# Mixing stage of a hybrid decoder block: norm sums placed among the u products, masks added once per bank, zero rows by DMA, a new order of steps

## The chip, the cores and the metric

One core of a Trainium2 chip runs the whole kernel in one launch. The metric is device time in microseconds of that core; less is better. TensorE multiplies, VectorE and ScalarE work on elements, GpSimd does some element work and issues DMAs, SyncE only issues DMAs. Each engine runs its own queue in order and waits on semaphores of the others.

## The reference

One layer of a decoder block on 512 tokens of width 1024, in float32, cut to what matters:

```python
h = h + 0.5 * swiglu(rmsnorm(h, norm_ffn1), w1, w3, w2)
z = rmsnorm(h, norm_mix) @ w_in          # q | k, v of three branches | gates | u
o = concat(nsa(q, k, v, gates), s5(u))   # attention of 8 heads, and a state-space mixer on u
h = h + o @ w_out
h = h + 0.5 * swiglu(rmsnorm(h, norm_ffn2), ...)
h = h + sigmoid(rmsnorm(h) @ w_gate) * (p @ w_ple)
out = rmsnorm(h, norm_final)
```

The attention has three branches over the same queries: compressed keys (31 blocks, made from k and v by a small network), selected blocks and a window. With 512 tokens the last two both see all earlier tokens, so each is a causal softmax over keys of its own. The three are weighted by gates. The S5 mixer is a linear recurrence over time in 32 groups of 16 channels.

## The kernel before

Activations lie transposed, features on the 128 partitions and the 512 tokens along the free axis. Each float32 product is made of three products of rounded parts (`hi`, `lo` of the weights, `xh`, `xl` of the activations). Weights come in units of 128 x 1024 from `wpack`, through a ring `raw` of four buffers. ScalarE casts a unit to `hi`, VectorE subtracts it for `lo` (`split`, line 143), and the ring of `hi` and `lo` has three buffers each. A unit of the input projection is 24 products of 512 columns (`proj`, line 745).

The first feed-forward layer ends with eight sums of `down`. Each adds into `h`, and `Norm.feed` (line 183) then makes `xh`, `xl` and the running sum of squares `acc` for the next norm. The norm itself is `rsqrt_steps` (line 256). TensorE sums `acc` over the partitions into a bank D; VectorE and GpSimd take the root (`ms`, `ri`, `nt`, with GpSimd's power); VectorE makes four diagonals `dg`; TensorE spreads them with `ones` into another bank D; VectorE copies that to `rb` (line 190). The norm's factor is applied after the projection, so u, q and k can be multiplied before it is known, as far as PSUM banks hold them: tags A to D, two banks each.

`mixer` (line 696) holds the mixing stage, about 378 to 662 us. It is made of generators, one for each strand of work:

- `s5_input` (u): four u units, finished with `rb` into `ut`, stored, and read back as `u8`
- `rotary` (q, Q, and in `keys` for k): two units, six VectorE operations in the single buffers `r1`, `rb1`, `r2`, `r3`, then two stores. `keys` reads the stored keys back as `kf` (two buffers under the tag `ra`, which other tiles share) and makes `KA` and `KB`
- `s5_all` (s): the recurrence, chunk by chunk; `s5_back` transposes pairs of chunks and copies them to `yt`
- `cmp_kv` (z), `cmp_all` (c): the compressed keys and values, stored, read back in windows (`cst`) and multiplied with their weights
- `v_gates` (v), `glu` (g), `out_half` (f, half of the output projection)
- `queries` (p): reads q of one block of 128 queries back as `qf` and makes `QA` and `QB`, whose rows 64 to 111 hold the row maxima later and zeros at first
- `scores` (t), `compressed` (x): scores with queries on the partitions, for maxima and sums. Keys are added by two products (`KA`, `KB`); a third, with the identity `identb` as the stationary operand, adds the mask (line 1069)
- `values` (V): scores again with keys on the partitions, exponentials, products with the values

`PLAN` (line 1355) is a list of letters. Each takes the next piece of its strand, and a digit names the query block. This sets the order in which pieces are written down. A scheduler then orders each engine's queue by estimated times, except for instructions that are pinned (`pinned`, line 123). `issue_after` keeps one instruction behind another.

Where the lines below need a letter of a table: `TQ` (line 1346) names the banks of q's products, `GT` the buffers of the gelu, which are `r1` and `r2` again.

Of the kernel before, what the change touches and what calls it, by code (L numbers as in the profile page):

```python
# [10 lines left out]
F32 = mybir.dt.float32  # L11
# [4 lines left out]
OP = mybir.AluOpType  # L16
# [60 lines left out]
def block_kernel(ctx: ExitStack, tc: tile.TileContext, a: dict, out: bass.AP):  # L77
# [618 lines left out]
    def mixer(ctx):  # L696
# [22 lines left out]
        nc.scalar.dma_start(w2, a["cmp_w2"])  # L719
        bglu = mp.tile([128, 4], F32, name="bglu")  # L720
        nc.scalar.dma_start(bglu, a["b_glu"])
        G.tensor_scalar(bglu, bglu, 0.5, None, OP.mult)

        for br in range(2):
            V.tensor_copy(KB[64:112, 2 * br:2 * br + 2, :],
                          orow[:, br + 1:br + 2, None].to_broadcast([48, 2, SEQ]))
        zero = mp.tile([128, 1], F32, name="zero")
        pad(mp, PADS[1])
        G.memset(zero, 0.0)
        tp = ctx.enter_context(tc.tile_pool(name="tmp", bufs=1, reuse_waits="tile"))  # L730
        s5x = ExitStack()
        s5w = s5x.enter_context(tc.tile_pool(name="s5w", bufs=2, reuse_waits="tile"))
        V.tensor_copy(KBc[64:112], orow[:, 0:1].to_broadcast([48, 160]))
        V.tensor_copy(VLc.rearrange("p g d -> p (g d)"), zero[:, 0:1].to_broadcast([128, 256]))
        V.tensor_copy(KAc, zero[:, 0:1].to_broadcast([128, 192]))
        V.tensor_copy(KBc[0:64], zero[0:64, 0:1].to_broadcast([64, 160]))


        at = {}
# [27 lines left out]


        def s5_input():
            for m in range(4):  # L770
                o = proj("u", TU[m % 2])
                if m == 0:
                    nm.finish()
                    for t, raw in zip((cosr, sinr), ropes):
                        V.tensor_tensor(t, raw, nm.rb, OP.mult)
                ut = mp.tile([128, 8, 64], F32, tag="ut", name="ut", bufs=2)
                V.tensor_tensor(ut.rearrange("p s c -> p c s"), o.rearrange("p (c s) -> p c s", s=8),
                                nm.rb.rearrange("p (c s) -> p c s", s=8), OP.mult)
                nc.sync.dma_start(ud[128 * m:128 * (m + 1)], ut)
# [253 lines left out]
        def queries(qb, pool):  # L1033

            tq = slice(qb * 128, (qb + 1) * 128)
            QA = pool.tile([128, 8, 128], FR, tag="QA", name="QA", bufs=2)
            QB = pool.tile([128, 8, 128], FR, tag="QB", name="QB", bufs=2)
            envs[qb].update(QA=QA, QB=QB)
            S.copy(QB[64:112].rearrange("p h q -> p (h q)"), zero[64:112, 0:1].to_broadcast([48, 1024]))
            for i, (hs, st) in enumerate(zip((slice(0, 4), slice(4, 8)), STAGE[qb])):  # L1040
                src = qd[i].rearrange("(h r) a t -> (r a) h t", h=4)[:, :, tq]
                if st == "ra":
                    qf = mp.tile([128, 4, 128], F32, tag=st, name="qf", bufs=2)
                else:
                    qf = tp.tile([128, 4, 128], F32, tag=st, name="qf")
                nc.sync.dma_start(qf[0:64], src)
                nc.sync.dma_start(qf[64:128], src)
                S.activation(QA[:, hs], qf, AF.Copy, scale=0.125)
                S.activation(QB[0:64, hs], qf[0:64], AF.Copy, scale=0.125)
                V.scalar_tensor_tensor(QA[64:128, hs], qf[64:128], 0.125, QA[64:128, hs].bitcast(F32),  # L1050
                                       OP.mult, OP.subtract)
                yield

        def scores(qb, tags="B"):

            nk = (qb + 1) * 128
# [292 lines left out]
GT = "r1", "r2"
# [2 lines left out]

PLAN = """u u u k u s s k s k s s s q q Q s k s Q s p3 t3 t3 s z t3 s s t3 z s t3 s s t3 t3 s p3 t3 s t3 g t3 g t3 t3 v
g v c t3 v c v c c c c p2 t2 t2 p2 t3 c t2 t3 t2 c t2 t3 c v t2 c t2 t2 t2 t2 t2 t2 t2 t2 g t2 t2 close p1 p1
p0 p0 x3 g g g g t1 t1 x2 S2 R3 V3 V3 V3 V3 V3 V3 f t1 t1 R2 t1 f t1 f x1 t1 V3 V3 V3 V3 V3 f V3 V3 V3 f t1 V3
V3 V3 V3 t0 V3 V2 f V2 t0 V2 V2 t0 V2 V2 t0 V2 V2 x0 f V2 V2 S0 R1 V2 R0 V2 V2 V2 f V2 V1 V1 V1 V1 V1 V1 V1 V1
V1 V1 V1 V0 V0 V0 V0 V0 V0 V0"""
DEBUG_STOP = None  # L1360
PADS = 320, 0, 224, 24832

# [150 lines left out]
```

## Time and profile before

| | us |
|---|---|
| median of three runs | 1076.79 (1075.64 to 1078.86) |
| the profiled execution's own time | 1076.96 |
| its span, first to last instruction | 1075.2 |
| TensorE busy in the span | 1042.5 |
| VectorE, ScalarE, GpSimd busy | 756.0, 459.4, 170.5 |

The span lies 1.8 us under the time of the same execution. PE in a row is TensorE's products, PEld its weight loads, DVE is VectorE, ACT ScalarE, POOL GpSimd, SP SyncE. A group of rows names the view it is from.

### The profile page before, as it was taken

The numbers are of one execution on the slowest core, as the hardware profiler recorded it, in microseconds if no ns is written. First come the engines' busy times: TensorE is split into PE (matmuls) and PEld (weight loads), VectorE is DVE, ScalarE is ACT, GpSimd is POOL, SyncE is SP. The second block draws the span as 40 slices with busy tenths as digits, with TensorE's granted clock in tenths as the row PEclk, the third lists the DMA queues.
The fourth block names the chain that finished last, engine by engine and source line by source line (L and its number), as shares of the span: only waits on it lengthen the run. The fifth ranks groups of instructions, "written<-read, shape, count | busy, mean of one in ns | idle before, by whom it ended". The sixth has DMA issues, their size and how long they took to land.

```text
span 1075.2 us, 14929 instructions
## 1 busy us (share of the span) xinstructions
PE 1042.5 (97%) x5782; PEld 872.3 (81%) x5782; DVE 756.0 (70%) x1271; ACT 459.4 (43%) x778; POOL 170.5 (16%) x191
## 2 busy tenths in 40 slices
PE   7999999999999989899999999999999999999995
PEld 5888888888888868676587668799899899899885
DVE  6995454545447857587678876997598679687666
ACT  6222223124222531337767865554256245245441
POOL 4006065425549411000000000000000000000000
PEclk9999999999999999998999999999999999999998
DMA  7333225326933938764612014333333323423402
GB/s 253 124 99 101 95 98 156 107 92 205 220 102 112 294 98 219 217 205 135 210 40 59 1 39 137 99 110 108 97 101 101 133 71 107 137 79 121 151 23 79
DMA packets 50391, 132.66 MB, mean 123 GB/s; under 512 B 10560, under 2 KB 17312, under 8 KB 50320
## 3 DMA queue, kind: packets, MB, share of 16 engines
q10 hardware_dynamic: 26080, 90.51, 26.5%
q0 software_dynamic: 6032, 21.79, 7.7%
q1 hardware_dynamic: 18208, 19.40, 6.0%
q8 instruction: 45, 0.74, 0.3%
q14 instruction: 26, 0.21, 0.1%
HBM read 114.09 MB, written 17.83 MB: 123 GB/s over the span
## 4 chain that ended last, share of the span: by engine, by line
PE 51%; DMA 4%; DVE 4%; issue 2%; ACT 1%; SPq 0%; POOL 0%; POOLq 0%; DVEq 0%; ACTq 0%
PE ps_A L126 15%; PE ps_C L126 14%; PE ps_D L126 12%; PE ps_B L126 11%; DMA qd<-r 1%; DMA raw<-in_wpack 1%; DMA kf<-kd 1%; DMA kd<-r 1%; DMA cst<-kcd 0%; DVE lo L150 0%; ACT e L758 0%; DMA qf<-qd 0%; DVE vv L819 0%; DVE ple L1304 0%; DVE xl L223 0%
## 5 line engine op out<-in xcount | busy, mean ns | idle before, releaser
L148 ACT CAST hi<-raw 128x1024 fp32r<-128x1024 f32 (+2 forms) x146 | 151.9, 1041 | 344.1 <-PE ps_C L126 123.3
L150 DVE TENSOR_TENSOR lo<-raw,hi 128x1024 fp32r<-128x1024 f32 (+2 forms) x146 | 188.9, 1295 | 60.8 <-ACT hi L148 60.0
L126 PE MATMUL ps_C<-hq,hi 128*128 128x512 f32 x704 | 217.3, 390 | 0.7 <-DVE h L405 0.7
L126 PEld LDWEIGHTS ps_C<-hq,hi 128*128 128x128 f32 x704 | 131.5, 188 | 28.3 <-DVE h L405 1.5
L126 PE MATMUL ps_C<-hq,lo 128*128 128x512 f32 x352 | 137.0, 389 | 0.0
L126 PE MATMUL ps_A<-xh,hi 128*128 128x512 f32 (+1 forms) x352 | 128.9, 366 | 6.2 <-ACT xh L171 6.2
L126 PE MATMUL ps_A<-xl,hi 128*128 128x512 f32 (+1 forms) x352 | 128.6, 365 | 1.5 <-DVE xl L223 0.8
L126 PE MATMUL ps_A<-xh,lo 128*128 128x512 f32 (+1 forms) x352 | 127.5, 362 | 0.0
L265 POOL TENSOR_TENSOR ri<-ms,negh 128x4 f32<-128x4 f32 (+1 forms) x6 | 6.6, 1104 | 597.3 <-DVE ms L264 597.3
L126 PE MATMUL ps_B<-xh,hi 128*128 128x512 f32 (+1 forms) x264 | 100.4, 380 | 0.9 <-ACT hi L148 0.9
L126 PE MATMUL ps_B<-xh,lo 128*128 128x512 f32 (+1 forms) x264 | 99.9, 378 | 0.0
L126 PE MATMUL ps_B<-xl,hi 128*128 128x512 f32 (+1 forms) x264 | 99.6, 377 | 0.0
L405 DVE SCALAR_TENSOR_TENSOR h<-ps_C,h 128x512 f32<-128x512 f32 x64 | 43.9, 689 | 56.2 <-PE ps_C L126 55.9
L126 PEld LDWEIGHTS ps_A<-xh,hi 128*128 128x128 f32 x352 | 67.0, 190 | 16.9 <-ACT xh L171 6.2
L148 ACT CAST hi<-s 128x1024 fp32r<-128x1024 f32 x40 | 42.1, 1053 | 86.8 <-PE ps_D L126 37.6
L126 PEld LDWEIGHTS ps_A<-xl,hi 128*128 128x128 f32 x352 | 67.0, 190 | 14.2 <-DVE xl L223 2.4
L126 PEld LDWEIGHTS ps_C<-hq,lo 128*128 128x128 f32 x352 | 66.1, 188 | 13.6
L126 PEld LDWEIGHTS ps_A<-xh,lo 128*128 128x128 f32 x352 | 67.0, 190 | 10.0
L150 DVE TENSOR_TENSOR lo<-s,hi 128x1024 fp32r<-128x1024 f32 x40 | 49.0, 1225 | 16.5 <-ACT hi L148 16.4
L126 PEld LDWEIGHTS ps_B<-xh,hi 128*128 128x128 f32 x264 | 49.7, 188 | 10.6 <-ACT hi L148 1.3
L126 PEld LDWEIGHTS ps_B<-xh,lo 128*128 128x128 f32 x264 | 49.7, 188 | 9.4 <-DVE lo L150 0.4
L126 PEld LDWEIGHTS ps_B<-xl,hi 128*128 128x128 f32 x264 | 49.7, 188 | 9.4 <-issue 0.4
(417 smaller groups left out, 2297.5 us busy)
## 6 DMA issues: line engine op xcount, KB each, us to landing
raw<-in_wpack ACTq DMA_DIRECT2D x168, 512.0 KB, 3.5
so<-s5o POOLq DMA_DIRECT2D x8, 768.0 KB, 5.9
si<-s5i POOLq DMA_DIRECT2D x8, 512.0 KB, 6.4
raw<-in_wpack SPq DMA_DIRECT2D x4, 512.0 KB, 6.7
h<-in_xT SPq DMA_DIRECT2D x8, 256.0 KB, 5.0
s5i<-fs POOLq DMA_DIRECT2D x1, 2048.0 KB, 11.7
s5o<-gt POOLq DMA_DIRECT2D x1, 2048.0 KB, 13.1
s5o<-gt POOLq DMA_DIRECT2D x2, 1024.0 KB, 19.0
```

What stands on the lines that cost most here:

```text
L126: return PE.matmul(o, lhsT, rhs, start=start, stop=stop, **kw)
L148: S.copy(hi[:, c], raw[:, c])
L150: V.tensor_tensor(lo[:, c], raw[:, c], hi[:, c].bitcast(F32), OP.subtract)
L265: G.tensor_tensor(ri, ms, negh[:, :nb], OP.pow)
L405: V.scalar_tensor_tensor(h[:, m, :], o, 0.5, h[:, m, :], OP.mult, OP.add)
```

## The change

It does six things. The sums of the mixing norm are emitted after the eighth k of the first u unit, and its broadcast after the sixth k of the second (`SUMS_U`, `CAST_U`, counted from 0), with all u products pinned in this order. The constant fills of the key and value tiles, and the scaling of `bglu` (now on VectorE), come behind the broadcast's copy. The mask products of a bank become one product over all its heads, in the scores of blocks 0 and 1 and in the compressed scores; the first key product of the bank alone starts it. For blocks 0 and 1 the zero rows of `QB` come by a DMA from GpSimd's queue out of zero rows of `VLc`, in place of a ScalarE copy. q's products lie in banks A instead of B. And `PLAN` is another list.

```diff
-        G.tensor_scalar(bglu, bglu, 0.5, None, OP.mult)
-        for br in range(2):
-            V.tensor_copy(KB[64:112, 2 * br:2 * br + 2, :], ...)
...
+        def fills():
+            for br in range(2):
+                V.tensor_copy(KB[64:112, 2 * br:2 * br + 2, :],
+                              orow[:, br + 1:br + 2, None].to_broadcast([48, 2, SEQ]))
+            V.tensor_scalar(bglu, bglu, 0.5, None, OP.mult)
+            V.tensor_copy(KBc[64:112], orow[:, 0:1].to_broadcast([48, 160]))
+            V.tensor_copy(VLc.rearrange("p g d -> p (g d)"), zero[:, 0:1].to_broadcast([128, 256]))
+            V.tensor_copy(KAc, zero[:, 0:1].to_broadcast([128, 192]))
+            V.tensor_copy(KBc[0:64], zero[0:64, 0:1].to_broadcast([64, 160]))
...
-        def proj(name, tag="A"):
+        def proj(name, tag="A", beside=None):
...
-                mm3(o, wu[0][:, sl], wu[1][:, sl], nm.xh[:, k, :], nm.xl[:, k, :], k == 0, k == KT - 1)
+                for j, (w_, x_) in enumerate(((0, nm.xh), (0, nm.xl), (1, nm.xh))):
+                    p = mm(o, wu[w_][:, sl], x_[:, k, :], k + j == 0, k == KT - 1 and j == 2)
+                    if beside is not None:
+                        pinned(p)
+                if beside and k in beside:
+                    beside[k]()
...
         def s5_input():
+            norm = rsqrt_steps([nm.acc], 4, True, True)
+            out = []
+            def spread():
+                nm.ri, pb = next(norm)
+                nm.rb = npool.tile([128, SEQ], F32, tag="rb", name="rb", bufs=1)
+                c = V.tensor_copy(nm.rb, pb)
+                for t, raw in zip((cosr, sinr), ropes):
+                    V.tensor_tensor(t, raw, nm.rb, OP.mult)
+                with tc.issue_after(c.ins):
+                    fills()
+            sides = {SUMS_U: lambda: next(norm)}, {CAST_U: spread}, {}, None
             for m in range(4):
-                o = proj("u", TU[m % 2])
-                if m == 0:
-                    nm.finish()
-                    for t, raw in zip((cosr, sinr), ropes):
-                        V.tensor_tensor(t, raw, nm.rb, OP.mult)
+                out.append(proj("u", TU[m % 2], sides[m]))
+                for i in (() if m == 0 else (0, 1) if m == 1 else (m,)):
...
-            S.copy(QB[64:112].rearrange("p h q -> p (h q)"), zero[64:112, 0:1].to_broadcast([48, 1024]))
+            if qb > 1:
+                S.copy(QB[64:112].rearrange("p h q -> p (h q)"), zero[64:112, 0:1].to_broadcast([48, 1024]))
+            else:
+                G.dma_start(QB[64:112].rearrange("p (a h) q -> p a (h q)", a=4),
+                            VLc[64:112].rearrange("p g d -> p (g d)")[:, None, :].to_broadcast([48, 4, 256]))
...
-                    mm(s_[:, i], QA[:, h0 + i], KAg[:, g, rs, :nk], True, False)
+                    mm(s_[:, i], QA[:, h0 + i], KAg[:, g, rs, :nk], i == 0, False)
                     mm(s_[:, i], QB[0:112, h0 + i], KBg[0:112, g, rs, :nk], False, False)
-                    mm(s_[:, i, :, nk - 128:], identb, maskq[:, None, :].to_broadcast([128, nb, 128]), False, True)
+                mm(s_[:, :, :, nk - 128:], identb, maskq[:, None, None, :].to_broadcast([128, n, nb, 128]), False, True)
...
-                    mm(sc[:, hd], QA[:, hd], KAc[:, 64 * g:64 * g + 64], True, False, skip_group_check=True)
-                    mm(sc[:, hd, 0], identb, cmq[:, qb], False, True, skip_group_check=True)
+                    mm(sc[:, hd], QA[:, hd], KAc[:, 64 * g:64 * g + 64], hd == 0, False, skip_group_check=True)
+                mm(sc[:, :, 0], identb, cmq[:, qb, None, :].to_broadcast([128, 8, 32]), False, True,
+                   skip_group_check=True)
...
+SUMS_U, CAST_U = 7, 5
-TU, TQ, TW, TY, TP = "AD", "BB", "C", "D", "D"
+TU, TQ, TW, TY, TP = "AD", "AA", "C", "D", "D"
-PLAN = """u u u k u s s k s k s s s q q Q s k s Q s p3 t3 t3 s z t3 s s t3 z s t3 s s t3 t3 s p3 t3 s t3 g t3 g t3 t3 v
+PLAN = """u u u k s s u k k q s q s Q p3 s s s k s Q s t3 t3 s t3 z t3 s s t3 s p3 s z t3 t3 s s t3 t3 s g t3 g t3 g t3
...
```

How this moves instructions is shown at three places.

**The norm, on TensorE and VectorE.** On TensorE before, with buffer numbers (`ps_A_3151` is the third u unit, `ps_D_3109` the second, `ps_D_3076` the sums, `ps_D_3094` the broadcast):

```order
L126 MATMUL ps_A_3151<-xh_2794,lo_3148 128x512
L126 MATMUL ps_D_3076<-ones_90,acc_2796 128x1 x4
L126 MATMUL ps_D_3094<-dg_3089,ones_90 128x512
L126 MATMUL ps_D_3109<-xh_2794,hi_3105 128x512
L126 MATMUL ps_D_3109<-xl_2795,hi_3105 128x512
```

Now (`ps_A_3044` is the first u unit, `ps_D_3093` the second, `ps_D_3069` the sums, `ps_D_3112` the broadcast):

```order
L126 MATMUL ps_A_3044<-xl_2795,hi_3040 128x512
L126 MATMUL ps_A_3044<-xh_2794,lo_3041 128x512
L126 MATMUL ps_D_3069<-ones_90,acc_2796 128x1 x4
L126 MATMUL ps_D_3093<-xh_2794,hi_3089 128x512
L126 MATMUL ps_D_3093<-xl_2795,hi_3089 128x512
L126 MATMUL ps_D_3093<-xh_2794,lo_3090 128x512
```

and 15 products of `ps_D_3093` later:

```order
L126 MATMUL ps_D_3093<-xl_2795,hi_3089 128x512
L126 MATMUL ps_D_3093<-xh_2794,lo_3090 128x512
L126 MATMUL ps_D_3112<-dg_3082,ones_90 128x512
L126 MATMUL ps_D_3093<-xh_2794,hi_3089 128x512
L126 MATMUL ps_D_3093<-xl_2795,hi_3089 128x512
```

The broadcast followed the sums with nothing between; now 18 products stand between them. On VectorE before (`ms` to `dg` are the norm, `KB<-orow` to `KAc<-zero` fills):

```order
L725 CAST KB<-orow 48x1024 x2
L733 CAST KBc<-orow 48x160
L181 TENSOR_TENSOR acc<-acc,sq 128x512
L734 CAST VLc<-zero 128x256
L735 CAST KAc<-zero 128x192
L736 CAST KBc<-zero 64x160
L150 TENSOR_TENSOR lo<-raw,hi 128x1024
L264 TENSOR_SCALAR ms<-ps_D 128x4
L150 TENSOR_TENSOR lo<-raw,hi 128x1024
L266 TENSOR_TENSOR nt<-ri 128x4
L267 SCALAR_TENSOR_TENSOR nt<-nt,ms 128x4
L268 SCALAR_TENSOR_TENSOR ri<-nt,ri 128x4
L271 TENSOR_SCALAR dg<-ident,ri 128x128 x4
L190 COPY rb<-ps_D 128x512
```

Now:

```order
L264 TENSOR_SCALAR ms<-ps_D 128x4
L266 TENSOR_TENSOR nt<-ri 128x4
L150 TENSOR_TENSOR lo<-raw,hi 128x1024
L267 SCALAR_TENSOR_TENSOR nt<-nt,ms 128x4
L268 SCALAR_TENSOR_TENSOR ri<-nt,ri 128x4
L271 TENSOR_SCALAR dg<-ident,ri 128x128 x4
L786 COPY rb<-ps_D 128x512
L733 CAST KB<-orow 48x1024 x2
L735 TENSOR_SCALAR bglu<-bglu 128x4
L736 CAST KBc<-orow 48x160
L737 CAST VLc<-zero 128x256
L738 CAST KAc<-zero 128x192
```

The split `lo` moved from ahead of `nt` to behind it, and the fills from ahead of the norm to behind `rb`; one more of them and the table `cosr` follow the last row.

**The rotation of the first q pair, on VectorE and SyncE.** On VectorE before (`r_3493`, `r_3495`, `rb_3494`, `r_3496` are the temporaries `r1`, `r2`, `rb1`, `r3` of that pair):

```order
L871 TENSOR_TENSOR r_3493<-ps_B,cosr 128x512
L872 TENSOR_TENSOR r_3495<-ps_B,sinr 128x512
L823 TENSOR_TENSOR z<-vv,si 128x8x63
L150 TENSOR_TENSOR lo<-raw,hi 128x1024
L889 TENSOR_TENSOR KB<-kf,KA 64x512
L873 TENSOR_TENSOR rb_3494<-ps_B,sinr 128x512
L874 TENSOR_TENSOR r_3496<-ps_B,cosr 128x512
L875 TENSOR_TENSOR r_3493<-r_3493,rb_3494 128x512
L150 TENSOR_TENSOR lo<-raw,hi 128x1024
L876 TENSOR_TENSOR r_3495<-r_3495,r_3496 128x512
L889 TENSOR_TENSOR KB<-kf,KA 64x512 x2
```

Now (the same four are `r_3425`, `r_3427`, `rb_3426`, `r_3428`; `t` are operations of S5):

```order
L891 TENSOR_TENSOR r_3425<-ps_A,cosr 128x512
L892 TENSOR_TENSOR r_3427<-ps_A,sinr 128x512
L893 TENSOR_TENSOR rb_3426<-ps_A,sinr 128x512
L894 TENSOR_TENSOR r_3428<-ps_A,cosr 128x512
L895 TENSOR_TENSOR r_3425<-r_3425,rb_3426 128x512
L833 TENSOR_TENSOR t_3446<-ps_C,si 128x256
L834 TENSOR_TENSOR t_3447<-ps_C,si 64x256
L835 TENSOR_TENSOR t_3447<-ps_C,si 64x256
L150 TENSOR_TENSOR lo<-raw,hi 128x1024
L896 TENSOR_TENSOR r_3427<-r_3427,r_3428 128x512
L909 TENSOR_TENSOR KB<-kf,KA 64x512 x2
```

The products with `KB` stood in the middle of the rotation and now stand behind it. On SyncE before, from the first keys that are read back (`qd<-r` stores q, `qf<-qd` reads it for a query block):

```order
L886 DMA kf<-kd 64x512
L887 DMA kf<-kd 64x512
L886 DMA kf<-kd 64x512
L887 DMA kf<-kd 64x512
L877 DMA qd<-r_3493 128x512
L878 DMA qd<-r_3495 128x512
L886 DMA kf<-kd 64x512
L887 DMA kf<-kd 64x512
L1046 DMA qf<-qd 64x4x128
L1047 DMA qf<-qd 64x4x128
```

Now:

```order
L906 DMA kf<-kd 64x512
L907 DMA kf<-kd 64x512
L897 DMA qd<-r_3425 128x512
L898 DMA qd<-r_3427 128x512
L1071 DMA qf<-qd 64x4x128
L1072 DMA qf<-qd 64x4x128
L906 DMA kf<-kd 64x512
L907 DMA kf<-kd 64x512
L906 DMA kf<-kd 64x512
L907 DMA kf<-kd 64x512
```

The stores and the reads of q moved ahead of the last two pairs of key reads.

**The second q pair, on SyncE.** Before (`r_3614`, `r_3616` are its temporaries, `kcd` the compressed keys' store, `cst` a window):

```order
L877 DMA qd<-r_3614 128x512
L878 DMA qd<-r_3616 128x512
L904 DMA kcd<-ra 64x512 x2
L940 DMA cst<-kcd 64x512
L1046 DMA qf<-qd 64x4x128
L1047 DMA qf<-qd 64x4x128
```

Now (the temporaries are `r_3623`, `r_3625`):

```order
L897 DMA qd<-r_3623 128x512
L898 DMA qd<-r_3625 128x512
L1071 DMA qf<-qd 64x4x128
L1072 DMA qf<-qd 64x4x128
L924 DMA kcd<-ra 64x512 x2
L960 DMA cst<-kcd 64x512
```

The read of `qf` moved from behind the store and the first window of the compressed keys to directly behind its own store.

## Rows read from the trace of the kernel before

**Rows 1.** The page's first part: busy time, share, instructions by engine

```profile
PE 1042.5 (97%) x5782; PEld 872.3 (81%) x5782; DVE 756.0 (70%) x1271; ACT 459.4 (43%) x778; POOL 170.5 (16%) x191
```

**Rows 2.** Windows: stretch, its us, busy us (count) by engine, PE clock, DMA, GB/s

```profile
388.40:392.30 3.90, 0.01 (x1) 0.00 (x0) 2.70 (x9) 0.07 (x1) 2.00 (x1) 1.00 0.64 161
392.30:396.20 3.90, 3.86 (x8) 2.45 (x9) 1.88 (x3) 0.00 (x0) 0.00 (x0) 0.56 0.29 112
404.00:444.00 40.00, 40.00 (x250) 32.91 (x249) 27.47 (x56) 8.25 (x12) 3.85 (x7) 1.00 0.87 227
455.00:461.00 6.00, 6.00 (x20) 4.52 (x21) 5.90 (x13) 0.68 (x3) 1.07 (x2) 0.52 0.44 132
489.00:495.00 6.00, 6.00 (x32) 4.18 (x33) 5.94 (x13) 5.14 (x13) 0.00 (x0) 0.51 0.29 88
580.00:633.00 53.00, 52.38 (x207) 32.91 (x205) 47.51 (x100) 45.64 (x89) 0.00 (x0) 1.00 0.07 21
```

**Rows 3.** TensorE's waits, 380 to 745: total us, times, longest

```profile
PE ps_B L126 <- DVE QA L1050: 4.2, 2, 3.8
PE ps_D L126 <- DVE dg L271: 3.9, 1, 3.9
PE ps_D L126 <- ACT yt L846: 1.9, 1, 1.9
...
PE ps_A L126 <- ACT oh L1179: 0.8, 1, 0.8
```

**Rows 4.** Timeline of VectorE at the norm: start, us, engine, line

```profile
381.37 1.29 DVE L725 CAST KB<-orow 48x1024 fp32r<-48x1024 f32 x2
382.58 0.23 DVE L733 CAST KBc<-orow 48x160 fp32r<-48x160 f32 x1
...
388.55 1.23 DVE L150 TENSOR_TENSOR lo<-raw,hi 128x1024 fp32r<-128x1024 f32 x1
...
395.02 0.69 DVE L775 TENSOR_TENSOR cosr<-rope,rb 128x512 f32<-128x512 f32 x1
...
396.23 1.08 DVE L777 TENSOR_TENSOR ut<-ps_A,rb 128x512 f32<-128x512 f32 x1
```

**Rows 5.** The chain that ended last, 400 to 468: start, us, what

```profile
401.45 5.44 PE ps_A L126 x24
...
423.89 6.35 DMA kd<-r
...
430.90 8.00 DMA kf<-kd
...
443.88 5.58 DMA qd<-r
...
450.20 3.23 DMA qf<-qd
...
460.33 7.58 DMA qd<-r
```

**Rows 6.** Timeline of VectorE around q's rotation and first QA

```profile
439.64 0.68 DVE L889 TENSOR_TENSOR KB<-kf,KA 64x512 fp32r<-64x512 f32 x1 [6.15 <-ACT KA L888]
...
454.11 0.69 DVE L1050 SCALAR_TENSOR_TENSOR QA<-qf,QA 64x512 fp32r<-64x512 f32 x1 [0.94 <-ACT QA L1048]
```

**Rows 7.** Timeline of ScalarE at the second read of q

```profile
483.55 0.63 ACT L1049 ACTIVATE QB<-qf 64x512 fp32r<-64x512 f32 x1 [3.80 <-DMA qf<-qd]
...
486.07 0.58 ACT L846 COPY yt<-ps_D 128x512 f32<-128x512 f32 x1
```

**Rows 8.** Timeline of TensorE: key products of the compressed scores

```profile
542.02 0.28 PE L126 MATMUL ps_B<-KAc,QA 128*128 128x64 f32 x1
...
542.17 0.28 PE L126 MATMUL ps_B<-KAc,QA 128*128 128x64 f32 x1
```

**Rows 9.** Timeline of VectorE: the last window sum

```profile
502.40 0.60 DVE L947 TENSOR_TENSOR sinr<-cst,pe 128x256 f32<-128x256 f32 x1
```

**Rows 10.** Timeline of TensorE: the first compression products

```profile
503.95 0.65 PE L126 MATMUL ps_A<-raw,cs 128*64 128x256 f32 x2
```

More of the change, by code (lines that the diff above doesn't have):

```diff
@@ L721, in mixer @@
         nc.scalar.dma_start(bglu, a["b_glu"])
-        G.tensor_scalar(bglu, bglu, 0.5, None, OP.mult)
-        for br in range(2):
-            V.tensor_copy(KB[64:112, 2 * br:2 * br + 2, :],
-                          orow[:, br + 1:br + 2, None].to_broadcast([48, 2, SEQ]))
         zero = mp.tile([128, 1], F32, name="zero")
@@ L732, in mixer @@
         s5w = s5x.enter_context(tc.tile_pool(name="s5w", bufs=2, reuse_waits="tile"))
[L733 to L736, printed above, removed]
+        def fills():
[7 more added lines that the diff above has]
+            V.tensor_copy(KBc[0:64], zero[0:64, 0:1].to_broadcast([64, 160]))
         at = {}
@@ L769, in s5_input @@
         def s5_input():
-            for m in range(4):
-                o = proj("u", TU[m % 2])
-                if m == 0:
-                    nm.finish()
-                    for t, raw in zip((cosr, sinr), ropes):
-                        V.tensor_tensor(t, raw, nm.rb, OP.mult)
[L776 to L779, printed above, removed]
+            norm = rsqrt_steps([nm.acc], 4, True, True)
[9 more added lines that the diff above has]
+            sides = {SUMS_U: lambda: next(norm)}, {CAST_U: spread}, {}, None
+            for m in range(4):
+                out.append(proj("u", TU[m % 2], sides[m]))
+                for i in (() if m == 0 else (0, 1) if m == 1 else (m,)):
+                    ut = mp.tile([128, 8, 64], F32, tag="ut", name="ut", bufs=2)
+                    V.tensor_tensor(ut.rearrange("p s c -> p c s"), out[i].rearrange("p (c s) -> p c s", s=8),
+                                    nm.rb.rearrange("p (c s) -> p c s", s=8), OP.mult)
+                    nc.sync.dma_start(ud[128 * i:128 * (i + 1)], ut)
                 if m % 2:
@@ L1350 @@
 STAGE = ("ra", "ra"), ("ra", "ra"), ("ra", "ra"), ("ra", "ra")
-PLAN = """u u u k u s s k s k s s s q q Q s k s Q s p3 t3 t3 s z t3 s s t3 z s t3 s s t3 t3 s p3 t3 s t3 g t3 g t3 t3 v
[L1356 to L1359, printed above, removed]
+PLAN = """u u u k s s u k k q s q s Q p3 s s s k s Q s t3 t3 s t3 z t3 s s t3 s p3 s z t3 t3 s s t3 t3 s g t3 g t3 g t3
+v t3 c v v c t3 v c c p2 t2 t3 t3 t2 p2 c c c t2 c c t2 t2 c v t2 t2 t2 t2 t2 t2 t2 t2 t2 g close p1 p1 p0 x3
+p0 g t2 g t2 g g t1 t1 x2 f S2 t1 f t1 t1 f t1 t1 f f t0 t0 R2 f x1 t0 R3 V3 V3 V3 V3 V3 V3 V3 V3 V3 V3 V3 V3
+V3 V3 V3 V3 x0 f V3 t1 V3 V3 V2 V2 V2 V2 V2 t0 V2 V2 V2 V2 V2 S0 V2 R1 R0 V2 V2 V2 f V2 V1 V1 V1 V1 V1 V1 V1
+V1 V1 V1 V1 V0 V0 V0 V0 V0 V0 V0"""
 DEBUG_STOP = None
```

## The prediction

> **What bounds the kernel now.** I read the busy line of the page first: TensorE is at work in 97% of the span, VectorE in 70%, ScalarE in 43% [rows 1]. So time can be won where TensorE stands still, where it runs at half speed, or by taking work off it. Next, the stretches by granted clock [rows 2]: in the mixing stage the clock is 1.00 except in three places. It is 0.56 in the 3.9 us after an idle stretch at 388.4, 0.52 in 455 to 461, and 0.51 in 489 to 495, which are the lower of the two levels (1.2 and 2.4 GHz) for nearly the whole stretch. Then TensorE's waits between 380 and 745 us [rows 3]: 3.9 us for `dg` of the norm, 4.2 in two waits for `QA` (3.8 of it in one), 1.9 for a copy `yt`, and little else. Each cold stretch follows one of these. The wait of 0.8 us for `oh` in the same rows leaves no cold stretch behind it. Last, the chain that ended last [rows 5], which shows why `QA` is late: keys go out to memory (6.35 us) and come back (8.00), q goes out (5.58) and comes back (3.23).
>
> **The change part by part.** The sum is made against the profiled execution's own time, 1076.96 us, which lies 0.2 above the median of the three runs.
>
> *Sums and broadcast among u's products.* Before, TensorE waits 3.9 us between the sums and the broadcast [rows 3]. Now 18 products of the second u unit stand between them. A unit of 24 takes 5.44 us [rows 5], so 18 take 4.1. But on VectorE a split `lo` (1.23 us) now stands inside the chain, behind `nt`; before, it ran beside GpSimd's power [rows 4]. The chain then takes at most 3.9 + 1.2 = 5.1 us, and 1.0 us of waiting is left; between 0 and 1.2. Gain 2.9. A wait that short cooled nothing in rows 3, so the cold stretch goes too: 3.9 us at 0.56 lose 3.9 x 0.44 = 1.7 us.
>
> *Fills moved.* Two key fills take 1.29 us together, and the five others I put at 0.23 each, the one shown [rows 4]: 2.4 us that lay beside the last down product now lie between the broadcast's copy `rb` and `cosr`. They delay what frees u's banks: after `rb` (0.69) come 2.4 of fills, two tables (1.4) and two `ut` (2.2), in all 6.7 us. TensorE meanwhile has the last 6 products of the second unit and the whole third unit, 30 x 0.227 = 6.8 us, before it needs the second unit's bank. I count nothing; the cover is that unit, and without it the price is 2.4 us. The scaling of `bglu` leaves GpSimd for VectorE and is one of the five.
>
> *q before k.* The rotation of the first q pair stood behind a `KB` that waited 6.15 us for keys coming back [rows 6]. Now it stands ahead of it, and on the DMA queue of SyncE the reads of q stand ahead of the last keys. Keys landed at 423.89 + 6.35 = 430.2; with the norm's part the keys are done about 5 us sooner, so 425. The temporaries `r1` and `r2` have one buffer each, so the rotation starts there: six operations of 0.69, a split of 1.23 and three small ones (under 0.69 each) end by 433 at the latest. Add 5.58 out, 0.7 of issue, 3.23 back: 442. From landing to the end of `QA` it was 1.4 us (453.4 to 454.8): 443 to 444. TensorE, with the same products ahead of the first score, began it right behind `QA` at 454.8 and now comes there at 454.8 - 2.9 - 1.7 - 3.8 = 446.4. So the wait should go with some 3 us in hand. Gain 3.8, and the cold stretch of 455 to 461 with it: 6.0 x 0.48 = 2.9. Bounds: all of the 6.7 kept, or all gone. I take all gone, since the slack is larger than the differences between landings of one kind.
>
> *The second q pair's read goes ahead of the compressed keys on SyncE.* Before, ScalarE stood 3.80 us for `qf` with the copy `yt` behind it, done at 486.7 only [rows 7]; that read was issued behind the stores of the compressed keys. Now it is issued right after its own store. TensorE's 1.9 for `yt` and the second wait for `QA` (4.2 - 3.8 = 0.4) go, and with them the cold stretch of 489 to 495, 6.0 x 0.49 = 2.9. Gain 5.2; bounds 0 and 5.2, and I take the upper end less the next term.
>
> *What is late next.* TensorE would reach the first compression product 2.9 + 1.7 + 3.8 + 2.9 + 5.2 = 16.5 us earlier, at 487.5 instead of 503.95 [rows 10]. The window sums that feed it ended at 503.0 [rows 9], so they had hardly 1 us in hand. Their chain runs through the store of the second q pair (460.33 + 7.58 = 467.9 before [rows 5]), whose buffers the gelu and the windows reuse. I place that store's landing at 459 to 460, since the last keys still come before it, 8 us sooner; with ScalarE's 3.8 us gone as well, the windows end 12 to 14 us sooner, near 490. So TensorE waits 2 to 4 us there, or in smaller pieces before it: I give back 3.0, bounds 0 to 6. For VectorE, at the same work in a shorter stage, I give back another 1.0.
>
> *Masks.* Of the products with the identity that add a mask, 8 fewer for block 1, 4 for block 0, 28 in the compressed scores: 40. The columns streamed stay the same. A pair of a 64-column key product and its 32-column mask takes 0.155 us [rows 8]. A saved one is worth at least nothing and at most half a pair, 0.08. I take 0.04 each, since the columns remain: 1.5 us in a stage that TensorE fills. Bounds 0 and 3.1. The Trainium skill (TensorE: Matmul & The Clock Gate, Back-to-back issue gap) says that sustained pairs of weight load and 128-column product come every 81 ns or so; by that figure 40 fewer would be an estimated 3.2 us. The pairs here agree with it as a pitch (0.155 for two), and that sum would be 1.7 us better than mine.
>
> *Zero rows by DMA.* Two ScalarE copies go, two DMAs from GpSimd's queue come. The copies were off TensorE's path, so I count nothing. The DMAs are last on that queue but for later norms, and the scores that read them stand behind the scores of block 2 and the GLU products, which hide them; a landing is 3.2 to 8.0 us here [rows 5].
>
> *The value stage.* In 580 to 633 VectorE is busy 47.5 of 53 us and ScalarE 45.6 [rows 2]. The order of its exponentials, differences and products is the same but for a few scores that stand earlier. Nothing, bounds 2 either way.
>
> **Sum.** -2.9 -1.7 (norm), -3.8 -2.9 (`QA`), -5.2 (`yt`), -1.5 (masks), +3.0 +1.0: -14.0. 1076.96 - 14.0 = 1063.0 us.
>
> **Rivals.**
> *Waits come back elsewhere.* The compression of the stage meets VectorE and the round trips through memory; only the norm's 4.6, the masks' 1.5 and some 1 us stay: 1070. For it: in 404 to 444 the DMA engines are busy for 0.87 of the time and VectorE for 27.5 of 40 us [rows 2], and both get the same work in less time. Against it: the reads were moved ahead of what held them.
> *More than forecast.* The windows keep up, masks pay double: 14.0 + 4.0 + 1.5 = 19.5 less, 1057.5.
> *Nothing to measure.* Each gain of the q part returns as a wait with a cold stretch behind it, as rows 2 and 3 show them in pairs (3.8 with 2.9, 1.9 with 2.9), and the norm's 4.6 go to the fills and the split: 1076.
> *Slower.* Keys out, keys back, q out, q back, last keys back, second q out, second q back are seven round trips in series, since the rotations share `r1` and `r2`. The same bytes now move in less time. Were each landing x longer, the stage would grow by 7x once the 3 us in hand are used; from x = 2.4 (14 + 3 over 7) on it is slower than before. A first store took 5.58 and the next 7.58 [rows 5], so x = 2 happens, though not on all seven; at x = 3.5 it gives 1063 + 21.5 = 1084.
> *The DMAs for the zero rows starve.* The Trainium skill (SBUF — State Buffer, Who interferes with whom) says that GpSimd cannot write a DMA's descriptors while VectorE holds the port pair that they share. Here GpSimd's queue and VectorE work side by side in the S5 stretch without TensorE waiting for it [rows 3]. If it held the two DMAs past the GLU, the first scores of block 1 would wait for a landing, 8.0 at the longest, and run cold for 2.9 after it: 1063 + 10.9 = 1074.
>
> **How the numbers follow.** About 0.3% (3 us) is what a measurement of this kernel tells from no change. Forecast, 1058 to 1067: 0.60. More than forecast: 0.10. Waits back elsewhere: 0.18. Nothing to measure, and the starved DMAs for their part within 3 us: 0.07. Slower: 0.05. Faster is 0.60 + 0.10 + 0.18 = 0.88, same 0.07, slower 0.05. The range takes the first three cases whole with their bounds, 1056 to 1072, and leaves out about 0.15.
>
> **What would show it.** Right: sums and broadcast with at most some 1 us of waiting between them and clock 1.00 behind; no wait for `QA` over 1 us; `QA`'s first half about 10 us earlier; ScalarE no longer waiting 3.8 us for `qf`; the first compression product near 490; 40 fewer mask products; the value stage as long as before. Wrong: a wait of several us at the third or fourth u unit (fills), a cold stretch anywhere between 390 and 500, or a value stage that is longer.

## The result, and the profile after

The changed kernel takes 1063.2 us (median of four runs, 1061.92 to 1064.05), the kernel before 1077.36 beside it: ratio 0.9868, 95% interval 0.9849 to 0.9887. Its profiled execution has a span of 1061.1 us against 1075.2. The prediction was 1063.0. That its sum came out is partly luck: four of its terms were off, and the errors nearly cancel. What each stage gave is read below.

The first part of the page, after, against [rows 1]:

```profile
PE 1035.4 (98%) x5742; PEld 868.7 (82%) x5742; DVE 757.5 (71%) x1272; ACT 457.1 (43%) x776; POOL 170.1 (16%) x192
```

TensorE has 40 products fewer, the masks. TensorE's waits, 380 to 745 us, after, against [rows 3]:

```profile
PE ps_C L126 <- ACT ps_C L767: 2.5, 1, 2.5
PE ps_D L126 <- DVE z L843: 1.0, 1, 1.0
...
PE ps_A L126 <- ACT oh L1205: 0.8, 1, 0.8
```

The waits for `dg`, `QA` and `yt` are gone. Two new ones are there, and `oh` is as long as before. The stretches by granted clock, after, against [rows 2]:

```profile
376.00:392.00 16.00, 16.00 (x75) 12.88 (x74) 10.40 (x25) 7.88 (x9) 1.05 (x1) 1.00 0.37 109
...
466.80:471.80 5.00, 4.98 (x24) 4.09 (x25) 4.83 (x12) 2.48 (x6) 0.00 (x0) 0.66 0.36 135
...
566.00:616.80 50.80, 50.31 (x200) 31.55 (x198) 45.40 (x93) 44.98 (x89) 0.00 (x0) 1.00 0.06 21
...
618.20:621.90 3.70, 3.70 (x9) 2.90 (x10) 1.66 (x5) 0.99 (x2) 0.00 (x0) 0.54 0.02 4
```

The norm's stretch (376 to 392) is full, at clock 1.00. Two stretches remain mostly at the lower level: one behind the wait for `ps_C`, one behind the wait for `oh`. They lose 5.0 x 0.34 = 1.7 and 3.7 x 0.46 = 1.7 us. The first of them is one of the prediction's own signs of being wrong, a cold stretch between 390 and 500.

The chain that ended last, after, against [rows 5]:

```profile
418.34 5.67 DMA kd<-r
...
424.66 3.01 DMA kf<-kd
...
430.87 3.27 DMA qd<-r
...
434.90 6.49 DMA qf<-qd
...
452.33 6.16 DMA qd<-r
```

The first q leaves at 430.87 in place of 443.88, the second at 452.33 in place of 460.33. The single landings changed both ways: the keys came back in 3.01 us in place of 8.00, and q came back in 6.49 in place of 3.23 [rows 5].

### The profile page after: what moved, and what is told of

Same layout as the page of the kernel before. It is cut to its first block, busy times and chain, and to the rows that moved or that the text cites. A ratio compares the mean times of both kernels' runs of the same rounds, so it can differ in the third digit from the quotient of the medians.

```text
span 1061.1 us, 14854 instructions
## 1 busy us (share of the span) xinstructions
PE 1035.4 (98%) x5742; PEld 868.7 (82%) x5742; DVE 757.5 (71%) x1272; ACT 457.1 (43%) x776; POOL 170.1 (16%) x192
## 4 chain that ended last, share of the span: by engine, by line
PE 90%; DVE 3%; DMA 3%; ACT 2%; issue 2%; SPq 0%; POOL 0%; POOLq 0%; ACTq 0%; DVEq 0%
PE ps_A L126 29%; PE ps_C L126 27%; PE ps_B L126 22%; PE ps_D L126 12%; DMA qd<-r 1%; DMA qf<-qd 1%; DMA kd<-r 1%; DMA raw<-in_wpack 0%; ACT e L767 0%; PE ps_D L590 0%; ACT xh L171 0%; DMA kf<-kd 0%; DVE ple L1330 0%; DVE xl L223 0%; ACT hi L148 0%
## 5 line engine op out<-in xcount | busy, mean ns | idle before, releaser
L126 PE MATMUL ps_A<-xh,hi 128*128 128x512 f32 (+1 forms) x384 | 141.6, 369 | 6.4 <-ACT xh L171 6.4
L126 PE MATMUL ps_A<-xl,hi 128*128 128x512 f32 (+1 forms) x384 | 141.5, 368 | 1.3 <-DVE xl L223 0.8
L126 PE MATMUL ps_A<-xh,lo 128*128 128x512 f32 (+1 forms) x384 | 140.6, 366 | 0.0
L126 PE MATMUL ps_B<-xh,hi 128*128 128x512 f32 (+1 forms) x232 | 87.7, 378 | 0.9 <-ACT hi L148 0.9
L126 PEld LDWEIGHTS ps_A<-xh,hi 128*128 128x128 f32 x384 | 73.1, 190 | 18.6 <-ACT xh L171 6.4
L126 PE MATMUL ps_B<-xh,lo 128*128 128x512 f32 (+1 forms) x232 | 87.2, 376 | 0.0
L126 PE MATMUL ps_B<-xl,hi 128*128 128x512 f32 (+1 forms) x232 | 87.0, 375 | 0.0
L126 PEld LDWEIGHTS ps_A<-xl,hi 128*128 128x128 f32 x384 | 73.0, 190 | 15.4 <-DVE xl L223 2.4
L126 PEld LDWEIGHTS ps_A<-xh,lo 128*128 128x128 f32 x384 | 73.2, 191 | 11.4
L126 PEld LDWEIGHTS ps_B<-xh,hi 128*128 128x128 f32 x232 | 43.7, 188 | 9.2 <-ACT hi L148 1.3
```

What stands on the lines that cost most here:

```text
L126: return PE.matmul(o, lhsT, rhs, start=start, stop=stop, **kw)
```

## The experiments

Each is timed against the kernel before on the same chip, so ratios are compared, with 95% intervals in brackets. The changed kernel has 0.9868 in the first set of runs and 0.9878 in a second. Differences of 2 us or less lie within these intervals, and there the traces have to decide.

**The norm alone.** The kernel before with the new `s5_input`, `proj` and `fills`; plan, masks and zero copies of before:

```diff
-                    nm.finish()
...
+            sides = {SUMS_U: lambda: next(norm)}, {CAST_U: spread}, {}, None
```

> The kernel before with the norm's part alone (sums after the eighth k of the first u unit, broadcast after the sixth k of the second, products pinned, fills behind the copy); plan, masks and zero copies of before. Theory, each gain stands by itself where the wait was: in the trace of the changed kernel the 3.9 us before the broadcast and the cold stretch behind it (1.7) are gone, and the keys go out sooner by as much, so the kernel is 5.6 us faster than before, ratio 0.9948, and the wait for QA stays at 3 to 5 us. Rival, the gain needs the new plan: QA hangs on round trips through memory that do not start sooner, and the wait for QA grows by what the norm saves: ratio 1.000, wait near 9 us.

Measured: 1071.34 us, ratio 0.9937 (0.9924 to 0.995). TensorE's waits in it:

```profile
PE ps_B L126 <- DVE QA L1070: 5.2, 2, 4.3
PE ps_D L126 <- ACT yt L866: 1.8, 1, 1.8
```

The wait for `dg` is gone, and those for `QA` and `yt` stay as they were within 1 us. So the gain stands where the wait was, and does not need the plan.

**The plan alone.**

```diff
-PLAN = """u u u k u s s k s k s s s q q Q s k s Q s p3 t3 t3 s z ...
+PLAN = """u u u k s s u k k q s q s Q p3 s s s k s Q s t3 t3 s t3 z ...
-TU, TQ, TW, TY, TP = "AD", "BB", "C", "D", "D"
+TU, TQ, TW, TY, TP = "AD", "AA", "C", "D", "D"
```

> The kernel before with the new plan and the banks A for q alone; norm, fills, masks and zero copies of before. Theory: the norm's wait and cold stretch (5.6) and the masks (2.0) are missing from the gain of 14.2, so 6.6 faster than before, ratio 0.994; no wait for QA over 1 us, a wait of some 2.5 us behind ScalarE near 468 us as in the changed kernel. Rival, the new order costs in the stage without the sooner keys: the waits come back, ratio 0.998 to 1.002.

Measured: 1070.32 us, ratio 0.9934 (0.9918 to 0.995). Its waits:

```profile
PE ps_D L126 <- DVE dg L271: 3.9, 1, 3.9
PE ps_C L126 <- ACT ps_C L758: 2.7, 1, 2.7
```

No wait for `QA` or `yt`, and the new one for `ps_C` comes with the plan. Norm and plan give 0.6 to 0.7% each, and their sum is the whole gain within the intervals.

**The masks per head again.**

```diff
-                    mm(s_[:, i], QA[:, h0 + i], KAg[:, g, rs, :nk], i == 0, False)
+                    mm(s_[:, i], QA[:, h0 + i], KAg[:, g, rs, :nk], True, False)
...
-                mm(s_[:, :, :, nk - 128:], identb, maskq[:, None, None, :].to_broadcast([128, n, nb, 128]), False, True)
+                    mm(s_[:, i, :, nk - 128:], identb, maskq[:, None, :].to_broadcast([128, nb, 128]), False, True)
```

and the same for `cmq`.

> The changed kernel with the mask products per head as before (40 more of them). Theory: 0.04 to 0.05 us each in a stage that TensorE fills, 1.5 to 2.0 us slower than the changed kernel, ratio to before 0.9885. Rival 1, they ran in the shadow of waits for VectorE and ScalarE: no slower, 0.987. Rival 2, each costs half a pair (0.08): 3.1 us slower, 0.990.

Measured: 1065.79 us (1063.36 to 1067.97), ratio 0.9885 (0.9869 to 0.9902). By the ratios this is 1.8 us above the changed kernel, and the intervals overlap: the time alone tells none of the three expectations from the others. The trace tells more. TensorE's timeline, after, of one compressed bank, one bank of block 1 and one bank of block 0:

```profile
534.01 1.06 PE L126 MATMUL ps_B<-KAc,QA 128*128 128x64 f32 x8
534.91 0.29 PE L126 MATMUL ps_B<-cmq,identb 128*128 128x256 bf16 x1
534.95 0.47 PE L126 MATMUL ps_C<-QA,KA 128*128 128x512 f32 x1
...
538.55 0.36 PE L126 MATMUL ps_B<-KA,QA 128*128 128x256 f32 x1
...
539.15 0.36 PE L126 MATMUL ps_B<-KA,QA 128*128 128x256 f32 x1
...
556.09 0.47 PE L126 MATMUL ps_B<-KA,QA 128*128 128x256 f32 x1
...
556.80 0.58 PE L126 MATMUL ps_C<-QB,KBc 112*128 112x512 f32 x1
```

and, of this experiment, one head of block 1, a compressed bank and a bank of block 0, each up to what follows it:

```profile
531.36 0.36 PE L126 MATMUL ps_A<-KA,QA 128*128 128x256 f32 x1
...
531.72 0.47 PE L126 MATMUL ps_A<-oh,hi 128*128 128x512 f32 x1
...
533.85 0.28 PE L126 MATMUL ps_B<-KAc,QA 128*128 128x64 f32 x1
...
535.10 0.47 PE L126 MATMUL ps_A<-oh,hi 128*128 128x512 f32 x1
...
543.77 0.36 PE L126 MATMUL ps_B<-KA,QA 128*128 128x256 f32 x1
...
544.50 0.28 PE L126 MATMUL ps_B<-KAc,QA 128*128 128x64 f32 x1
```

A compressed bank takes 534.95 - 534.01 = 0.94 us with one mask and 535.10 - 533.85 = 1.25 with eight, so each of the seven saved is worth 0.044, and four banks save 1.2. In block 1 a head with its own mask takes 0.36, two 0.72; a bank of two heads with one mask takes 539.15 - 538.55 = 0.60. The eight masks saved there are worth 0.12 each, 1.0 together. In block 0 a bank takes 0.71 with one mask and 0.73 with two: next to nothing. Together some 2.3 us.

**The broadcast early.** `SUMS_U, CAST_U = 7, 0` in place of `7, 5`.

> The changed kernel with the broadcast after the first k of the second u unit, so that 3 products stand between sums and broadcast in place of 18. Theory: the chain over VectorE and GpSimd takes 4.0 us from the sums (383.2 to 387.0), 0.7 of it covered, so a wait of 3.3 us comes back, or 2.1 if the split is not in the chain, with a cold stretch behind it that costs some 1.7: 4 to 5 us slower than the changed kernel, ratio to before 0.991. Rival, the keys and q have slack behind the norm: less than 2 us slower, 0.988, since QA and z are waited for less.

Measured: 1069.44 us, ratio 0.9912 (0.9898 to 0.9927). Its wait and its stretch by clock:

```profile
PE ps_D L126 <- DVE dg L271: 3.2, 1, 3.2
```

```profile
386.70:391.00 4.30, 3.88 (x9) 2.50 (x10) 2.04 (x5) 0.00 (x0) 0.00 (x0) 0.60 0.41 126
```

By the ratios this is 4.7 us slower than the changed kernel. The wait of 3.2 us comes back, and 4.3 x 0.40 = 1.7 at the lower level behind it; the profiled span is 5.0 longer. So what hides the chain is the 18 products, and the cold stretch belongs to the wait.

**The fourth exponential first.** Second half of `QA` and `QB`, and the gelu, behind the maximum and exponential of the fourth scores of block 3:

```diff
+                with tc.issue_after(marks[3][1].ins) if qb == 3 and i else nullcontext():
                     S.activation(QA[:, hs], qf, AF.Copy, scale=0.125)
                     S.activation(QB[0:64, hs], qf[0:64], AF.Copy, scale=0.125)
...
+                with tc.issue_after(marks[3][0].ins), tc.issue_after(marks[3][1].ins):
                     gelu2(yt, yt, SEQ, GT[m % 2])
```

> The changed kernel with two sets of ScalarE and VectorE operations put behind the maximum and the exponential of the fourth scores of block 3: the second half of QA and QB on ScalarE, and the gelu on both. In the changed kernel that exponential stood behind them, ScalarE waited for a store of q and for its reading back, and TensorE waited 2.5 us for the bank with some 1.7 us lost at half clock behind it. Theory: both go, 4 us faster than the changed kernel, 1059, ratio to before 0.983. Rival, something else is late right behind it (the later scores, the windows, the third and fourth QA): the wait moves and the time stays, 0.987.

Measured: 1063.05 us, ratio 0.9865 (0.9841 to 0.9889): the rival, no difference from the changed kernel. Its waits:

```profile
PE ps_A L126 <- issue: 3.0, 1, 3.0
...
PE ps_C L126 <- ACT ps_C L1102: 0.9, 2, 0.7
```

and VectorE, ahead of the first compression product, which came at 492.02:

```profile
489.72 0.58 DVE L967 TENSOR_TENSOR cosr<-cst,pe 128x256 f32<-128x256 f32 x1 [3.77 <-DMA cst<-vcd]
...
491.30 0.48 DVE L948 SCALAR_TENSOR_TENSOR VL<-ps_A,ri,VL 128x256 fp32r<-128x256 f32 x1
```

The wait for `ps_C` went down from 2.5 to 0.9 in two pieces, and a wait came back at the windows: TensorE stood 3.0 us ahead of the first compression product, and the 5 us behind it ran at 0.66. VectorE had stood 3.77 us for the last window's landing, with `VL` behind it, which empties bank A for the compression.

**Only QA and QB behind it.** The first half of that diff alone.

> The changed kernel with the second half of QA and QB alone put behind the exponential of the fourth scores of block 3 on ScalarE; the gelu stays ahead of it, so the stores, the windows and SyncE's order stay as in the changed kernel. Theory: that exponential comes right behind its maximum (463.3 in the changed kernel, against 466.0), TensorE waits for its bank by 0.1 us and not 2.5, and the cold stretch behind it (1.7) goes: 4 us faster than the changed kernel, 1059, ratio to before 0.983. Rival, as with the gelu moved too: the next thing (second half of QA, the windows) is late by as much, ratio 0.987.

Measured: 1061.27 us (1060.47 to 1062.81), ratio 0.9854 (0.9841 to 0.9868), the changed kernel beside it 1063.98 (1063.74 to 1064.39). Its waits:

```profile
PE ps_C L126 <- ACT ps_C L1101: 1.6, 3, 0.9
PE ps_A L126 <- issue: 1.3, 1, 1.3
```

and its clock over the stretch in which the changed kernel ran cold:

```profile
440.00:500.00 60.00, 57.02 (x412) 43.78 (x410) 51.60 (x104) 35.73 (x80) 4.41 (x8) 1.00 0.69 213
```

2.7 us better than the changed kernel beside it, and no run of one reaches the other; by the ratio of the first set it is 1.5. The cold stretch is gone. Less than the 4 expected came: waits of 1.6 in all, 0.9 at the longest, stayed at bank C, and 1.3 came back ahead of the compression, where ScalarE and VectorE had yet to empty bank A of the products of v; the windows were done by then. This has the lowest median of the versions run, level with the next one.

**The same with the fills ahead of the norm, and the changed kernel again.**

> The same, with the fills ahead of the norm as well. Theory: ahead of the norm the fills lie in a stretch that waits for the last sum of the first layer, and in the trace of the kernel with that edit alone the wait of 1.0 us for z was gone; at most 1 us faster than the same without it, ratio to before 0.982. Rival: no difference, 0.983.

Measured: 1061.39 us, ratio 0.9853 (0.9837 to 0.9868): no difference.

> The changed kernel as it is, beside the other two on the same chip. Both theories: ratio to before 0.987. In the trace: the wait of 2.5 us for the bank C near 464 and the one of 1.0 for z again; the wait of 0.8 us for oh at the end of the values again, with or without a stretch at half clock behind it, which came in one of the runs and not in others.

Measured: 1063.98 us, ratio 0.9878 (0.9864 to 0.9891). Waits as expected, 1.7 us for `z` this time. Behind bank C and behind `oh`:

```profile
467.00:477.00 10.00, 9.42 (x39) 6.78 (x39) 9.32 (x21) 4.79 (x12) 0.00 (x0) 0.66 0.45 153
619.00:625.00 6.00, 5.08 (x21) 3.77 (x22) 3.18 (x8) 1.45 (x4) 0.00 (x0) 1.00 0.01 3
```

Behind bank C, 10.0 x 0.34 = 3.4 us are lost, where the first profile of the same kernel lost 1.7 behind the same wait of 2.5. Behind `oh` the clock is 1.00, where the first profile had 0.54 behind the same wait of 0.8 us.

**Fills early, and zero rows by copies**, each alone in the changed kernel:

```diff
+        fills()
...
-                with tc.issue_after(c.ins):
-                    fills()
```

```diff
-            if qb > 1:
-                S.copy(QB[64:112].rearrange("p h q -> p (h q)"), zero[64:112, 0:1].to_broadcast([48, 1024]))
-            else:
-                G.dma_start(QB[64:112].rearrange("p (a h) q -> p a (h q)", a=4), ...)
+            S.copy(QB[64:112].rearrange("p h q -> p (h q)"), zero[64:112, 0:1].to_broadcast([48, 1024]))
```

> The changed kernel with the seven fills ahead of the norm as before, none behind the broadcast's copy. Theory: the third u unit covered them where they were, and 1 us of slack was left, so no difference, ratio to before 0.987. Rival 1, ahead of the norm they delay the running sum that the sums wait for: up to 2.4 us slower, 0.989. Rival 2, behind the copy they had pushed ut, u's stores and so the S5 chain: up to 2 us faster, 0.985.

> The changed kernel with the zero rows of QB of blocks 0 and 1 by ScalarE copies as before, no DMA from GpSimd's queue. Theory: neither is on TensorE's path, no difference from the changed kernel, ratio to before 0.987. Rival, two copies of 1.04 us on ScalarE lie ahead of the exponentials that free banks: 1 to 2 us slower, 0.9885.

Measured: 1062.73 us, 0.9866 (0.9842 to 0.989), and 1061.98 us, 0.986 (0.9833 to 0.9887). Neither can be told from the changed kernel, with intervals of about 2.5 us to either side.

**The last sum of the first half behind the values.** The last `f` of the plan at its end, its 12 products held behind the last product of the values:

```diff
+                    with tc.issue_after(state["po"].ins) if m == 7 and not done else nullcontext():
                         mm3(o, wu[0][:, sl], wu[1][:, sl], oh[:, k], ol[:, k], j == 0, j == n - 1)
```

> The changed kernel with the last of the eight sums of the first half of the output projection (12 products, 2.7 us) put behind the last product of the values, where TensorE waited 0.8 us for oh and, in the profiled run of the changed kernel but not in that of before, lost some 1.6 us at half clock behind it. Theory: TensorE was kept by VectorE and ScalarE where these products stood, so they cost nothing more at the end, and wait and cold stretch go: 1 to 2.5 us faster than the changed kernel, ratio to before 0.985. Rival, the products filled idle time where they stood: the value stage is no shorter and the 2.7 us come on top less the 0.8, 2 us slower, 0.9886.

Measured: 1064.91 us, ratio 0.9874 (0.9849 to 0.9899). The interval holds the forecast and its rival, so the time shows no gain and no loss. The trace shows the wait for `oh` gone, and the last product of the values, which now stands ahead of the 12, waits in its place:

```profile
PE ps_D L126 <- DVE el L1195: 1.1, 1, 1.1
```

The 6 us from 619 run at 0.72, so 1.7 us at the lower level did not go either.

**Work beside GpSimd's power.** See the last section for what it asks:

```diff
+        for _ in range(2 if beside is not None else 0):
+            pinned(V.tensor_tensor(beside, parts[0], parts[0], OP.subtract))
```

> The changed kernel with two VectorE subtractions of 128x512 (0.69 each, the result is overwritten and unused) between ms and nt, so that they run beside GpSimd's power as a split did before the change. Theory: GpSimd is held by VectorE meanwhile, so the power takes some 2.0 us as in the trace of before, not 1.05, the chain from the sums to dg is about 1 us longer, and TensorE waits up to 0.9 us for the broadcast; the time is 0 to 1 us more, ratio to before 0.988. Rival, the power of before was slow for another cause (a long idle GpSimd, its first use in this form): it stays at 1.05 and the chain is longer by 0.2 at most, what the two subtractions reach beyond it; ratio 0.987.

Measured: 1065.65 us, ratio 0.9874 (0.9849 to 0.9898), not told from the changed kernel.

## Why the prediction was right, and where its steps were not

**Norm: right, and 1.0 us undersized.** The prediction gave 2.9 + 1.7 and left 1.0 of waiting, since a split stood in the chain. Nothing was left. VectorE after:

```profile
383.18 0.16 DVE L264 TENSOR_SCALAR ms<-ps_D 128x4 f32<-128x4 f32 x1 [2.87 <-PE ps_D L126]
384.51 0.16 DVE L266 TENSOR_TENSOR nt<-ri 128x4 f32<-128x4 f32 x1 [1.17 <-POOL ri L265]
384.60 1.23 DVE L150 TENSOR_TENSOR lo<-raw,hi 128x1024 fp32r<-128x1024 f32 x1
...
386.13 0.88 DVE L271 TENSOR_SCALAR dg<-ident,ri 128x128 f32<-128x128 f32 x4
```

The chain takes 387.0 - 383.2 = 3.8 us with the split in it, where the prediction had 5.1 at most, and 18 products cover 4.1. The prediction held the power at its length of before; it took 1.05 us and not 2.00, which paid for the split. The run of the norm alone gave 0.0063 x 1078.0 = 6.8 us (5.4 to 8.2); the trace 3.9 + 1.7 = 5.6.

**Fills, zero rows: right at nothing**, as far as the two runs that undo them can tell. The rival of the starved DMAs fell too: the two were issued at 485.1 and 485.7 and landed in 4.7 us, some 35 us ahead of the first scores of block 1.

**q before k: right in time by luck, one thing missed.** `QA` ended at 442.8 against 443 to 444, and the first scores began at 446.10 against 446.4. The steps to it were off by more and cancel: q left 2 us sooner than forecast, its store took 3.27 us and not 5.58, and the read back took 6.49 and not 3.23. And VectorE had stood 4.28 us for `QA`, with the operations of S5 up to `z` behind it:

```profile
442.07 0.69 DVE L1075 SCALAR_TENSOR_TENSOR QA<-qf,QA 64x512 fp32r<-64x512 f32 x1 [4.28 <-ACT QA L1073]
...
444.12 0.68 DVE L843 TENSOR_TENSOR z<-vv,si 128x504 f32<-128x504 f32 x1
```

```profile
444.86 0.66 PE L126 MATMUL ps_D<-so,z 128*64 128x128 f32 x8 [1.01 <-DVE z L843]
```

TensorE waited 1.0 us for `z`, 1.7 in the second profile. How long it waits hangs on that one landing: in five profiles of the experiments on the changed kernel `QA` began by 441.3 in place of 442.07, and TensorE did not wait for `z` at all. The prediction gave back 1.0 for VectorE at the same work in a shorter stage. The size agrees, but it should have named the queue: who stands behind a waiting `QA` on VectorE.

**What is late next: the size about right, the place wrong.** This step failed as it was put: the windows. They ended at 487.59 + 0.60 = 488.2, and the first compression product began at 492.53 (the prediction had it near 490), with more than 4 us in hand. VectorE and TensorE, after:

```profile
487.59 0.60 DVE L967 TENSOR_TENSOR sinr<-cst,pe 128x256 f32<-128x256 f32 x1
```

```profile
492.53 0.43 PE L126 MATMUL ps_A<-raw,cs 128*64 128x256 f32 x1
```

The place was bank C, behind ScalarE:

```profile
458.56 1.20 ACT L767 ACTIVATE gt<-yt 128x512 f32<-128x512 f32 x2 [1.73 <-DMA qd<-r]
...
463.65 0.63 ACT L1074 ACTIVATE QB<-qf 64x512 fp32r<-64x512 f32 x1 [2.58 <-DMA qf<-qd]
...
465.99 0.66 ACT L767 ACTIVATE ps_C<-ps_C,nmax 128x512 f32<-128x512 f32 x1
```

The second q's store came at 452.33 + 6.16 = 458.5 (459 to 460 was said), and ScalarE still waited 2.58 for its reading back, where 3.80 had been. Behind it no longer stood `yt` but the exponential that frees bank C: 2.5 us of waiting and 1.7 cold, 4.2 where 3.0 was given back (2.5 and 3.4 in the second profile). The run with only `QA` and `QB` behind that exponential shows this cause: the wait falls, the cold stretch goes, and the kernel is faster. The run with the gelu moved as well shows that the windows can be the next thing, as the prediction had them first.

**Masks: mis-sized.** 0.04 each was taken, 0.08 at most. By the rows the 28 of the compressed scores are worth 0.044 each, as was taken; the 8 of block 1 are worth 0.12 each, above the bound; the 4 of block 0 next to nothing. That makes some 2.3 us where 1.5 was forecast. Why a saved mask is worth more in one place than in another was not tried. The Trainium skill (TensorE: Matmul & The Clock Gate, Back-to-back issue gap), by whose 81 ns the estimate had been 3.2, is off by about as much to the other side, and no group of the masks comes at 0.081.

**Value stage: right in its body, not behind it.** TensorE is busy 50.31 of 50.8 us, as it was 52.38 of 53 [rows 2]. Behind the unchanged wait for `oh`, 1.7 us were lost at half clock in the profiled run, where before lost nothing behind the same wait and the prediction expected nothing; the second profile had none.

**The sum.** By the first profile of each kernel: norm 5.6; `QA` 6.7 less 1.0 for `z`, 5.7; `yt` and the second `QA` 1.9 + 0.4 + 2.9 less 4.2 at bank C, 1.0; masks 2.3; lost behind `oh` 1.7. That is 5.6 + 5.7 + 1.0 + 2.3 - 1.7 = 12.9 of the 14.1 between the spans. Of the other 1.2, some 0.5 is idle time of TensorE in short pieces: over the stage (380 to 640 before, 380 to 626 after) it fell from 11.9 to 4.9 us, by 7.0, where the waits named here make 6.5. The rest was not traced to a place. Against the prediction, norm and masks gave 1.8 more; bank C and the clock behind `oh` took 2.9. A profile is one execution: in the second, `z` and bank C cost more and `oh` less.

Of the rivals, "waits come back elsewhere" happened in part. "Slower" did not come near: on the chain of this profile stores and reads of keys and q took 3.0 to 6.5 us, where before had 3.2 to 8.0 [rows 5].

## What to carry to other kernels

A wait of TensorE costs its length. Behind every wait of 1.8 us or more in the mixing stage of these profiles, another 1.7 to 3.4 us were lost at half clock, and behind some shorter ones too. Products that are ready anyway, put between the two ends of a round trip over other engines, took away both here.

Where a wait for memory moves, look at the operation that stands next behind it in the same engine's queue: `yt`, then an exponential, then a window took that place here in turn. Moving one thing forward then pays only part of the wait. Here moving two copies gave 1.5 to 2.7 us, and moving the gelu with them could not be told from the changed kernel, so it is worth trying the smallest move by itself.

## What the runs showed that was not expected

GpSimd's power on 128x4 takes 2.00 us in before, where a VectorE subtraction of two SBUF operands (the split) ran beside it, and 1.05 in the changed kernel, where none did. The run of the plan alone, with the split beside it, has 2.00 again, and the run of the norm alone 1.05. GpSimd's timeline of before, of after, and with two subtractions put beside it:

```profile
388.69 2.00 POOL L265 TENSOR_TENSOR ri<-ms,negh 128x4 f32<-128x4 f32 x1 [5.84 <-DVE ms L264]
```

```profile
383.43 1.05 POOL L265 TENSOR_TENSOR ri<-ms,negh 128x4 f32<-128x4 f32 x1 [14.15 <-DVE ms L264]
```

```profile
383.35 1.43 POOL L265 TENSOR_TENSOR ri<-ms,negh 128x4 f32<-128x4 f32 x1 [13.79 <-DVE ms L264]
```

So VectorE's work beside it costs GpSimd time, 0.4 us here. The Trainium skill (SBUF — State Buffer, Who interferes with whom) says that a VectorE operation with two SBUF inputs contends with a GpSimd operation that reads SBUF; this run agrees. The whole 0.95 did not come back; whether the split's longer rows or its operands make the rest was not tried. The chain was 0.4 us longer in that run, and the 18 products no longer covered it quite:

```profile
PE ps_D L126 <- DVE dg L273: 0.2, 1, 0.2
```

The clock behind a short wait is not settled by the wait's length. After 0.8 us for `oh` one profile of the changed kernel had 3.7 us at 0.54, another 1.00. After 1.7 us for `z` the second profile of the changed kernel stayed at 1.00 (the run with the last sum behind the values had 0.72 over the 6 us from 445). What decides it stays open, and with 1.7 us at stake it can be part of the spread between runs.
